# Weights that stream past the tokens: another matmul form for four products of a decoder layer

## The chip, the cores and the metric

The kernel runs on one core of a Trainium2 chip. The metric is the device time of one execution in microseconds (us), as the median of several runs. The core's engines work side by side, each through its own list of instructions in order: TensorE (PE) multiplies, VectorE (DVE) and ScalarE (ACT) do elementwise work, GpSimd (POOL) too, and SyncE (SP) issues most transfers from memory. Engines wait for each other by semaphores alone.

## The reference

One decoder layer for 256 tokens of 2048 features, in float32. A combined projection of the tokens gives the inputs of two branches and two merge gates; both branches are projected back, gated, added, projected once more and normalised:

```python
proj = x @ w_in        # columns: q_lat, c_kv, attn_gate, q_idx, k_idx, w_idx, x_rnn, rnn_gate, g_a, g_b
attn = sparse_attention(q_lat, rmsnorm(c_kv), q_idx, k_idx, w_idx, rel_bias, w_uv)   # 64 keys of each query
branch_a = (attn * silu(attn_gate)) @ w_branch_a
h = rglru(conv4(x_rnn), ...)                                                        # a scan over the tokens
branch_b = (h * silu(rnn_gate)) @ w_branch_b
merged = sigmoid(g_a) * branch_a + sigmoid(g_b) * branch_b
out = layernorm(2 ** 0.25 * x + merged @ w_out, ln_g, ln_b)
```

Here g_a and g_b are 2048 columns each, and w_branch_a, w_branch_b and w_out are 2048 x 2048.

## The kernel before, in words

Every large matrix product is made of float32 values split in two: a high part (`hi_of`, line 84, on ACT: a rounded copy) and the rest, the low part (`lo_of`, line 87, on DVE: value minus high part). A product is high x high + high x low + low x high. The tokens' two parts stand side by side in `xs`: for each of 16 blocks of 128 features, 256 columns of high parts and 256 of low ones.

The kernel has three phases. In the first, `load_a` and `split_a` (lines 223 and 234) bring the tokens and 848 columns of weights in 16 steps k, and PE multiplies as they come. In the second, `col_jobs` (line 51) lists 132 tiles of 128 weight columns: qi (indexer queries), ag (attention gate), q (latent queries), ga (gate A), ba (branch A's product), xr, gb, rg, bb (branch B's product). The weights of a tile come as two halves of 512 KB; `load_to` and `split_to` run some halves ahead, with 4 buffers for raw halves and 5 for split ones. In a tile the 128 weight columns are the stationary operand and the tokens move: a matmul with the weights' high part moves 512 columns (both halves of `xs`), one with the low part 256. `mm12` (line 192) issues a quarter of a tile, 4 of the 16 feature blocks: high first in the even quarters, low first in the odd ones. The result has features on the partitions and its two halves still have to be added, by `evac`: a copy on ACT, an addition on DVE.

After each quarter, a "tick", `tick` runs what is due of the work between the products: it is written as generators (`post_ga`, `post_bb`, `head`, `scores`, ...) which are called again some ticks later, so their instructions stand among the others of each engine at fixed places. `rel` copies a 4 MB table of position biases, dz, in the gate stage.

In the third phase the output projection has the other form: the tokens are stationary, 512 weight columns move, and `products` (line 781) issues three matmuls of 512 columns for one feature block and one half of the tokens. The result has tokens on the partitions. Its tiles are pso for the first three quarters of the columns, psz for the last one, which is done for one half of the tokens after the other, for the second half in two pieces of 256. `residual` adds the layer's input and `normalise` (line 800) finishes the norm of 128 tokens: the root of the variance by `rsqrt`, then `centre` (minus mean, times gain) and `finish` (times root, plus bias), with a quarter of the columns on ACT and POOL.

Of the kernel before, what the change touches and what calls it, by code (L numbers as in the profile page):

```python
# [49 lines left out]

def col_jobs():
# [12 lines left out]
def layer(ctx, tc, ar, out):  # L64
    nc = tc.nc
    jobs = col_jobs()
    NJ = len(jobs)
    at = {j: i for i, j in enumerate(jobs)}
# [34 lines left out]
    def gate_tile(name):  # L103
        return gt.tile([P, T], F32, name=name, tag="gate", bufs=32)
# [36 lines left out]

    halves = [("t", j, s) for j in range(NJ) for s in range(2)]
    halves += [("o", ec, pc) for ec in range(4) for pc in range(8)]
    NO = 2 * NJ
# [3 lines left out]
    def load_to(n):  # L148
        while st["load"] < min(n, len(halves)):
# [33 lines left out]
    def mm3(ps, hi, lo, rhs, first, last):  # L183

        if last:
            nc.tensor.matmul(ps[:, :T], lo, rhs[:, :T], start=first, stop=False)
            nc.tensor.matmul(ps, hi, rhs, start=False, stop=True)
        else:
            nc.tensor.matmul(ps, hi, rhs, start=first, stop=False)  # L189
            nc.tensor.matmul(ps[:, :T], lo, rhs[:, :T], start=False, stop=False)  # L190

    def mm12(ps, hi, lo, rhs, qt):


        def some(w, cols):
            for k in range(4 * qt, 4 * qt + 4):
                c = slice((k % 8) * P, (k % 8 + 1) * P)
                nc.tensor.matmul(ps[:, :cols], w[:, c], rhs[k][:, :cols], start=k == 0 and w is hi,  # L198
                                 stop=k == KT - 1 and w is hi)

        order = [(hi, 2 * T), (lo, T)]
        for w, cols in order if qt % 2 == 0 else order[::-1]:
            some(w, cols)
# [16 lines left out]
    with pool("pha", side="right") as pha:  # L220
# [13 lines left out]
        def split_a(k):  # L234
# [12 lines left out]
        nc.gpsimd.dma_start(params, ar["params"])  # L247
        nc.gpsimd.dma_start(causal, ar["causal"])
        nc.gpsimd.dma_start(kvg, ar["kvg"].to_broadcast([P, DL]))
        nc.gpsimd.dma_start(relb, ar["relb"])  # L250
        sp = {0: split_a(0)}
        for k in range(KT):
            if k + 1 < KT:
                sp[k + 1] = split_a(k + 1)
            if k + 4 < KT:
                load_a(k + 4)
            else:
                load_to(st["load"] + 1)
            hi, lo = sp.pop(k)
# [8 lines left out]
            for i in range(4):  # L268
                c = slice(A_Q + i * P, A_Q + (i + 1) * P)
                mm3(psq[i], hi[:, c], lo[:, c], xs[:, k, :], *fl)  # L270
# [214 lines left out]
    def head(h):  # L485
# [56 lines left out]
        nc.vector.tensor_mul(u, s, gates.pop(("ag", h)))  # L542
# [9 lines left out]
    def post_ag(i, ps):  # L552
        g = gate_tile(f"ag{i}")
        s = yield from evac(ps, f"ag{i}")
        yield
        nc.scalar.activation(g, s, AF.Sigmoid)
        yield
        nc.gpsimd.tensor_mul(g, g, s)
        gates["ag", i] = g

    def post_ga(i, ps):
        g = gate_tile(f"ga{i}")
        s = yield from evac(ps, f"ga{i}")
        yield
        nc.scalar.activation(g, s, AF.Sigmoid)
        gates["ga", i] = g

    def post_gb(i, ps):
        g = gate_tile(f"gb{i}")
        yield from evac(ps, f"gb{i}", dst=g)  # L570
        gates["gb", i] = g

    def post_ba(d, ps):
        s = yield from evac(ps, f"ba{d}")
        g = gates["ga", d]
        nc.vector.tensor_mul(g, g, s)

    def post_bb(d, ps):
        g = gates.pop(("gb", d))
        nc.scalar.activation(g, g, AF.Sigmoid)  # L580
        s = yield from evac(ps, f"bb{d}")
        yield
        nc.vector.tensor_mul(g, g, s)
        nc.vector.tensor_add(g, g, gates.pop(("ga", d)))
        yield
        hi_of(xs[:, d, :T], g)
        yield
        lo_of(xs[:, d, T:], g, xs[:, d, :T])
# [121 lines left out]
    E0, D0, A0, C0, G0 = (4 * at[k, 0] for k in ("ag", "q", "ga", "xr", "gb"))  # L710
# [19 lines left out]
    FIN = 4 * at["bb", 4]  # L730


    for j, (kind, i) in enumerate(jobs):
        rhs = us if kind in ("ba", "bb") else {k: xs[:, k, :] for k in range(KT)}
        ps = acc_tile(f"ps_{kind}{i}")
        for qt in range(4):
            t = 4 * j + qt
# [21 lines left out]
            hi, lo = parts[t // 2]  # L759
            mm12(ps, hi, lo, rhs, qt)  # L760
# [6 lines left out]
        spawn(4 * j + 4, posts[kind](i, ps))  # L767
# [31 lines left out]

    def normalise(t, ne):  # L800
# [31 lines left out]
        finish(cuts[0])  # L832
        centre(cuts[2])
        finish(cuts[1])
        centre(cuts[3])
        finish(cuts[2])
        finish(cuts[3])
# [82 lines left out]
```

## Time and profile before

| | |
|---|---|
| time, median of 3 runs | 1042.71 us (1040.66 to 1043.19) |
| the profiled execution | 1039.67 us, of which the span is 1037.8 us |
| PE busy | 1021.8 us, 98% of the span |
| DVE, ACT, POOL busy | 68%, 55%, 8% |
| mean granted clock of PE | 0.997 of full speed |
| transfers | 201 MB, mean 194 GB/s |

The span runs from the first instruction to the last. A matmul's length in the timeline is from its start to its result; since matmuls overlap, the pace is read from start to start. A row of the timeline can hold several equal instructions (x8). The bracket at a row's end is the idle time of the engine before it and what ended it.

### The profile page before, as it was taken

To read this page: it belongs to the slowest core of one execution; us is meant where nothing else is said; L and a number is where in the kernel's file an instruction comes from. 1 tells how busy PE (TensorE), PEld (TensorE's weight loads), DVE (VectorE), ACT (ScalarE), POOL (GpSimd) and SP (SyncE) were. 2 spreads that over 40 slices of the span, in tenths; PEclk is the share of its full clock that TensorE was granted. 3 is DMA by queue.
4 is the path that set the end of the run, shared out by engine and by line. 5 is a ranking of instruction groups with operands and counts; after the bars stand their busy time and mean duration, and the time that the engine had idled before them with its cause. 6 is when DMAs were issued, how large, how long until landed. Compare 5 with 4: busy or idle time off the path is not lost.

```text
span 1037.8 us, 16087 instructions
## 1 busy us (share of the span) xinstructions
PE 1021.8 (98%) x5944; PEld 901.4 (87%) x5944; DVE 709.8 (68%) x1246; ACT 571.1 (55%) x989; POOL 86.3 (8%) x121
## 2 busy tenths in 40 slices
PE   8999999999999999999999999999999999999995
PEld 8888888888898888888888888888888888888885
DVE  5668587777676766554555788856578877675666
ACT  5566355655656557544444555578755545554441
POOL 1003211211011100000000000000230020000002
PEclk9999999999999999999999999999999999999998
DMA  9745856755656654666665666556566577666642
GB/s 290 249 145 178 288 178 218 248 178 177 191 167 191 183 169 146 195 190 186 186 196 185 222 186 193 169 176 189 180 190 194 189 275 263 193 185 196 192 159 81
DMA packets 60574, 201.49 MB, mean 194 GB/s; under 512 B 6576, under 2 KB 13616, under 8 KB 59856
## 3 DMA queue, kind: packets, MB, share of 16 engines
q1 hardware_dynamic: 59120, 190.89, 59.1%
q0 software_dynamic: 944, 8.88, 2.3%
q8 instruction: 47, 0.77, 0.3%
q10 hardware_dynamic: 432, 0.70, 0.2%
q14 instruction: 31, 0.25, 0.1%
HBM read 198.31 MB, written 6.32 MB: 197 GB/s over the span
## 4 chain that ended last, share of the span: by engine, by line
PE 92%; DMA 3%; DVE 2%; ACT 1%; issue 1%; POOL 0%; SPq 0%; DVEq 0%; ACTq 0%; POOLq 0%
PE ps_q L198 17%; PE ps_ga L198 9%; PE ps_bb L198 9%; PE ps_rg L198 9%; PE ps_ba L198 9%; PE ps_gb L198 9%; PE ps_xr L198 9%; PE ps_ag L198 4%; DMA raw<-in_wt 3%; PE ps_qi L198 2%; PE pso L788 2%; PE pso L787 2%; PE pso L786 2%; ACT hi L85 1%; PE psq L189 1%
## 5 line engine op out<-in xcount | busy, mean ns | idle before, releaser
L89 DVE TENSOR_TENSOR lo<-raw,hi 128x1024 fp32r<-128x1024 f32 x324 | 401.3, 1239 | 290.7 <-ACT hi L85 289.4
L85 ACT ACTIVATE hi<-raw 128x1024 fp32r<-128x1024 f32 x324 | 340.7, 1052 | 104.0 <-PE pso L788 29.3
L198 PE MATMUL ps_q<-xs,hi 128*128 128x512 f32 x512 | 133.6, 394 | 0.0
L198 PEld LDWEIGHTS ps_q<-xs,hi 128*128 128x128 f32 x512 | 90.2, 189 | 14.2
L198 PEld LDWEIGHTS ps_q<-xs,lo 128*128 128x128 f32 x512 | 70.6, 190 | 5.1
L198 PE MATMUL ps_q<-xs,lo 128*128 128x256 f32 x512 | 73.5, 282 | 0.0
L198 PE MATMUL ps_ag<-xs,hi 128*128 128x512 f32 x256 | 66.1, 394 | 0.0
L198 PE MATMUL ps_ga<-xs,hi 128*128 128x512 f32 x256 | 65.5, 393 | 0.0
L198 PE MATMUL ps_gb<-xs,hi 128*128 128x512 f32 x256 | 64.4, 392 | 0.0
L198 PE MATMUL ps_rg<-xs,hi 128*128 128x512 f32 x256 | 64.3, 392 | 0.0
L198 PE MATMUL ps_ba<-ua,hi 128*128 128x512 f32 x256 | 64.3, 392 | 0.0
L198 PE MATMUL ps_bb<-ub,hi 128*128 128x512 f32 x256 | 64.3, 392 | 0.0
L198 PE MATMUL ps_xr<-xs,hi 128*128 128x512 f32 x256 | 64.0, 391 | 0.0
L198 PEld LDWEIGHTS ps_rg<-xs,hi 128*128 128x128 f32 x256 | 46.0, 189 | 8.2
L198 PEld LDWEIGHTS ps_bb<-ub,hi 128*128 128x128 f32 x256 | 46.0, 189 | 8.2
L198 PEld LDWEIGHTS ps_ba<-ua,hi 128*128 128x128 f32 x256 | 46.0, 189 | 8.2
L198 PEld LDWEIGHTS ps_gb<-xs,hi 128*128 128x128 f32 x256 | 46.0, 189 | 8.2
L198 PEld LDWEIGHTS ps_xr<-xs,hi 128*128 128x128 f32 x256 | 46.0, 188 | 8.0
L198 PEld LDWEIGHTS ps_ag<-xs,hi 128*128 128x128 f32 x256 | 45.3, 189 | 8.5 <-issue 0.9
L198 PEld LDWEIGHTS ps_ga<-xs,hi 128*128 128x128 f32 x256 | 45.6, 189 | 7.7
L442 POOL TENSOR_TENSOR bias<-bias,mask 128x256 f32<-128x256 f32 (+1 forms) x32 | 25.9, 830 | 174.8 <-DMA bias<-dz 136.2
L198 PEld LDWEIGHTS ps_xr<-xs,lo 128*128 128x128 f32 x256 | 35.8, 190 | 2.5
(270 smaller groups left out, 1810.2 us busy)
## 6 DMA issues: line engine op xcount, KB each, us to landing
raw<-in_wt SPq DMA_DIRECT2D x296, 512.0 KB, 4.3
raw<-in_wo SPq DMA_DIRECT2D x32, 512.0 KB, 3.6
wr<-in_wA SPq DMA_DIRECT2D x15, 424.0 KB, 4.8
dz<-dv POOLq DMA_DIRECT2D x1, 4096.0 KB, 18.3
bias<-dz SPq DMA_DIRECT2D x16, 256.0 KB, 4.5
xr<-in_xT SPq DMA_DIRECT2D x16, 128.0 KB, 4.3
uvr<-in_wuv SPq DMA_DIRECT2D x8, 256.0 KB, 4.2
wgr<-in_wg SPq DMA_DIRECT2D x4, 512.0 KB, 4.6
```

The source lines that it names most:

```text
L85: nc.scalar.activation(hi, src, AF.Copy)
L89: nc.vector.tensor_sub(lo, src, f(hi))
L189: nc.tensor.matmul(ps, hi, rhs, start=first, stop=False)
L198: nc.tensor.matmul(ps[:, :cols], w[:, c], rhs[k][:, :cols], start=k == 0 and w is hi, stop=k == KT - 1 and w is hi)
L442: nc.gpsimd.tensor_add(b[:, r, :W[r]], b[:, r, :W[r]], mask[:, r, :W[r]])
L786: nc.tensor.matmul(o, mh, hi, start=d == 0, stop=False)
L787: nc.tensor.matmul(o, mh, lo, start=False, stop=False)
L788: nc.tensor.matmul(o, ml, hi, start=False, stop=d == KT - 1)
```

## The change

The products ga, ba, gb and bb become 4 jobs of 512 columns each (`CHUNKS`), in the output projection's form: a job is 16 ticks, and a tick is one feature block with three matmuls for each half of the tokens. Their results have tokens on the partitions and need no halves added: `post_ga` takes the sigmoid straight from PSUM. What bb makes has to be turned for the output projection: `post_bb` has 8 transposes for each job on PE, and then the split into `xs`. The tiles that are left issue 8 high, 8 low, 8 low, 8 high matmuls (`mm`). Gate B stands ahead of rg as one block, and rg directly ahead of bb.

In the first phase four small loads (params 64 KB, causal 256 KB, kvg 128 KB, relb 2 KB) go from POOL's queue at the start to SP's at k = 8 to 11, the split of k = 1 and 2 is done in two pieces like that of k = 0, and the four 128-column products of a step take 4 high, then 4 low matmuls. In the third phase the residual of the second 128 tokens is written into PSUM in place and read there by the norm, which takes its columns in the pieces of the projection.

```diff
-    jobs += [("ga", i) for i in range(16)] + [("ba", i) for i in range(16)]
+    jobs += [("ga", i) for i in range(4)] + [("ba", i) for i in range(4)]
     jobs += [("xr", i) for i in range(16)]
-    jobs += [("gb", i) for i in range(14)] + [("rg", i) for i in range(16)] + [("gb", 14), ("gb", 15)]
-    jobs += [("bb", i) for i in range(16)]
+    jobs += [("gb", i) for i in range(4)] + [("rg", i) for i in range(16)]
+    jobs += [("bb", i) for i in range(4)]
...
-            for c in ([slice(0, A_Q), slice(A_Q, NA)] if k == 0 else [slice(0, NA)]):
+            for c in ([slice(0, A_Q), slice(A_Q, NA)] if k < 3 else [slice(0, NA)]):
...
-        nc.gpsimd.dma_start(params, ar["params"])
-        nc.gpsimd.dma_start(causal, ar["causal"])
-        nc.gpsimd.dma_start(kvg, ar["kvg"].to_broadcast([P, DL]))
-        nc.gpsimd.dma_start(relb, ar["relb"])
+        smalls = [(params, ar["params"]), (causal, ar["causal"]), (kvg, ar["kvg"].to_broadcast([P, DL])),
+                  (relb, ar["relb"])]
...
+            if 8 <= k < 12:
+                nc.sync.dma_start(*smalls[k - 8])
...
+    def post_ga(i, pss):
+        for t in range(2):
+            g = gates["ga", i, t] = gate_tile(f"ga{i}_{t}")
+            nc.scalar.activation(g, pss[t], AF.Sigmoid)
+            yield
...
+    def post_bb(i, pss):
+
+        gs = [gates.pop(("gb", i, t)) for t in range(2)]
+        for t in range(2):
+            nc.vector.tensor_mul(gs[t], gs[t], pss[t])
+            nc.vector.tensor_add(gs[t], gs[t], gates.pop(("ga", i, t)))
+            yield
+        yield
+        for e in range(2):
+            ps = aux_tile(f"psm{i}_{e}").rearrange("p (d s) -> p d s", d=2)
+            for d in range(2):
+                for t in range(2):
+                    c = slice((2 * e + d) * P, (2 * e + d + 1) * P)
+                    nc.tensor.transpose(ps[:, d, t * P:(t + 1) * P], gs[t][:, c], ident)
+            yield
+            d = slice(4 * i + 2 * e, 4 * i + 2 * e + 2)
+            hi_of(xs[:, d, :T], ps)
+            lo_of(xs[:, d, T:], ps, xs[:, d, :T])
...
+            if chunk:
+                for e in range(2):
+                    products(ps[e], parts[t // 2], qt % 2, qt, rhs[qt], e)
+            else:
+                high = qt in (0, 3)
+                w = parts[t // 2][0 if high else 1]
+                for kk in range(8):
+                    k = qt // 2 * 8 + kk
+                    mm(ps, w[:, kk * P:(kk + 1) * P], xs[:, k, :], high, k == 0 and high, k == KT - 1 and high)
...
     def residual(t, c, e, ps):
-        nc.vector.scalar_tensor_tensor(y[t][:, c], y[t][:, c], ALPHA, ps, op0=OP.mult, op1=OP.add)
-        nc.vector.bn_stats(st6[t][:, e, :], y[t][:, c])
+
+        to = ps if t else y[t][:, c]
+        nc.vector.scalar_tensor_tensor(to, y[t][:, c], ALPHA, ps, op0=OP.mult, op1=OP.add)
+        nc.vector.bn_stats(st6[t][:, e, :], to)
+        rows.append((t, c, to))
```

A tile on PE, in the xr stage (xr2 is its third tile, hi172 and lo172 the two parts of its first half of weights, x8 eight of a row). Before:

```order
L198 MATMUL ps_xr2_6327<-xs_93,hi172_6235 128x512 x4
L198 MATMUL ps_xr2_6327<-xs_93,lo172_6236 128x256 x8
L198 MATMUL ps_xr2_6327<-xs_93,hi172_6235 128x512 x4
L198 MATMUL ps_xr2_6327<-xs_93,hi173_6260 128x512 x4
L198 MATMUL ps_xr2_6327<-xs_93,lo173_6261 128x256 x8
L198 MATMUL ps_xr2_6327<-xs_93,hi173_6260 128x512 x4
```

and now:

```order
L203 MATMUL ps_xr2_5899<-xs_93,hi172_5809 128x512 x8
L203 MATMUL ps_xr2_5899<-xs_93,lo172_5810 128x256 x8
L203 MATMUL ps_xr2_5899<-xs_93,lo173_5833 128x256 x8
L203 MATMUL ps_xr2_5899<-xs_93,hi173_5832 128x512 x8
L203 MATMUL ps_xr3_5963<-xs_93,hi174_5859 128x512 x8
```

The two runs of low matmuls now stand together, and with the next tile so do two runs of high ones.

The bb stage on PE. Before, at its first tile (ub0 to ub7 are the scan's gated results of feature blocks 0 to 7, the moving operand; hi264 and lo264 the weights, stationary):

```order
L198 MATMUL ps_bb0_9172<-ub0_8275,hi264_9073 128x512
L198 MATMUL ps_bb0_9172<-ub1_8333,hi264_9073 128x512
L198 MATMUL ps_bb0_9172<-ub2_8391,hi264_9073 128x512
L198 MATMUL ps_bb0_9172<-ub3_8449,hi264_9073 128x512
L198 MATMUL ps_bb0_9172<-ub0_8275,lo264_9074 128x256
L198 MATMUL ps_bb0_9172<-ub1_8333,lo264_9074 128x256
L198 MATMUL ps_bb0_9172<-ub2_8391,lo264_9074 128x256
L198 MATMUL ps_bb0_9172<-ub3_8449,lo264_9074 128x256
L198 MATMUL ps_bb0_9172<-ub4_8507,lo264_9074 128x256
L198 MATMUL ps_bb0_9172<-ub5_8565,lo264_9074 128x256
L198 MATMUL ps_bb0_9172<-ub6_8623,lo264_9074 128x256
L198 MATMUL ps_bb0_9172<-ub7_8681,lo264_9074 128x256
```

Now, in the second job, where the first job's transposes stand (psm0_0; gb0_0 and gb0_1 are the gated sums of the first job for the two halves of the tokens):

```order
L756 MATMUL ps_bb1_1_8713<-hi273_8664,ub3_7935 128x512
L757 MATMUL ps_bb1_1_8713<-lo273_8665,ub3_7935 128x512
L758 MATMUL ps_bb1_1_8713<-hi273_8664,ub3_7935 128x512
L601 MATMUL psm0_0_8766<-ident_81,gb0_0_7093 128x128
L601 MATMUL psm0_0_8766<-ident_81,gb0_1_7109 128x128
L601 MATMUL psm0_0_8766<-ident_81,gb0_0_7093 128x128
L601 MATMUL psm0_0_8766<-ident_81,gb0_1_7109 128x128
L756 MATMUL ps_bb1_0_8712<-hi274_8682,ub4_7993 128x512
L757 MATMUL ps_bb1_0_8712<-lo274_8683,ub4_7993 128x512
L758 MATMUL ps_bb1_0_8712<-hi274_8682,ub4_7993 128x512
L756 MATMUL ps_bb1_1_8713<-hi274_8682,ub4_7993 128x512
L757 MATMUL ps_bb1_1_8713<-lo274_8683,ub4_7993 128x512
```

The weights are the moving operand now, the low matmuls have 512 columns too, and four transposes stand between two steps.

The last norm on DVE, second half of the tokens (mv1 holds mean and variance, lt1 the root, gb0 and gb1 gain and bias, y1 the rows in SBUF). Before, from the first centre on:

```order
L810 SCALAR_TENSOR_TENSOR y1_9388<-y1_9388,mv1_10045,gb0_9389 128x384
L290 RECIPROCAL lt1_10047<-lt1_10047 128x1
L810 SCALAR_TENSOR_TENSOR y1_9388<-y1_9388,mv1_10045,gb0_9389 128x512
L292 TENSOR_TENSOR lt1_10047<-lt1_10047 128x1
L293 TENSOR_TENSOR lt1_10047<-lt1_10047 128x1
L294 SCALAR_TENSOR_TENSOR lt1_10047<-lt1_10047 128x1
L814 SCALAR_TENSOR_TENSOR y1_9388<-y1_9388,lt1_10047,gb1_9390 128x384
L810 SCALAR_TENSOR_TENSOR y1_9388<-y1_9388,mv1_10045,gb0_9389 128x384
L814 SCALAR_TENSOR_TENSOR y1_9388<-y1_9388,lt1_10047,gb1_9390 128x512
L810 SCALAR_TENSOR_TENSOR y1_9388<-y1_9388,mv1_10045,gb0_9389 128x256
L814 SCALAR_TENSOR_TENSOR y1_9388<-y1_9388,lt1_10047,gb1_9390 128x384
L814 SCALAR_TENSOR_TENSOR y1_9388<-y1_9388,lt1_10047,gb1_9390 128x256
```

and now:

```order
L836 SCALAR_TENSOR_TENSOR pso0_1_9229<-pso0_1_9229,mv1_9225,gb0_8720 128x512
L292 RECIPROCAL lt1_9227<-lt1_9227 128x1
L294 TENSOR_TENSOR lt1_9227<-lt1_9227 128x1
L295 TENSOR_TENSOR lt1_9227<-lt1_9227 128x1
L296 SCALAR_TENSOR_TENSOR lt1_9227<-lt1_9227 128x1
L839 SCALAR_TENSOR_TENSOR y1_8719<-pso0_1_9229,lt1_9227,gb1_8721 128x512
L836 SCALAR_TENSOR_TENSOR pso1_1_9394<-pso1_1_9394,mv1_9225,gb0_8720 128x512
L839 SCALAR_TENSOR_TENSOR y1_8719<-pso1_1_9394,lt1_9227,gb1_8721 128x512
L836 SCALAR_TENSOR_TENSOR psz1_0_9802<-psz1_0_9802,mv1_9225,gb0_8720 128x256
L839 SCALAR_TENSOR_TENSOR y1_8719<-psz1_0_9802,lt1_9227,gb1_8721 128x256
L836 SCALAR_TENSOR_TENSOR psz1_1_9853<-psz1_1_9853,mv1_9225,gb0_8720 128x256
L839 SCALAR_TENSOR_TENSOR y1_8719<-psz1_1_9853,lt1_9227,gb1_8721 128x256
```

The rows are read from the projection's own PSUM tiles (pso0_1, pso1_1, psz1_0, psz1_1), and after the first piece each finish stands right behind its centre.

## Rows read from the trace of the kernel before

**Rows 1.** The page: busy time of each engine, and the chain by engine.

```profile
PE 1021.8 (98%) x5944; PEld 901.4 (87%) x5944; DVE 709.8 (68%) x1246; ACT 571.1 (55%) x989; POOL 86.3 (8%) x121
...
PE 92%; DMA 3%; DVE 2%; ACT 1%; issue 1%; POOL 0%; SPq 0%; DVEq 0%; ACTq 0%; POOLq 0%
```

**Rows 2.** Timeline of PE in the bb stage: start us, length us, operation, count.

```profile
881.78 2.00 PE L198 MATMUL ps_bb<-ub,hi 128*128 128x512 f32 x8
...
883.62 1.12 PE L198 MATMUL ps_bb<-ub,lo 128*128 128x256 f32 x8
...
926.47 2.00 PE L198 MATMUL ps_bb<-ub,hi 128*128 128x512 f32 x8
```

**Rows 3.** Tile pso on PE: duration min/median/max ns, first and last start.

```profile
L786 PE MATMUL pso<-hi,xs x96: 389/389/393, 938.6 to 1003.2; 128*128 128x512 f32 x96
...
L788 PE MATMUL pso<-hi,xs x96: 389/389/389, 939.0 to 1003.6; 128*128 128x512 f32 x96
```

**Rows 4.** Timeline of PE in the ga stage, around three transposes.

```profile
403.39 0.27 PE L517 MATMUL pspT<-ident,lg 128*128 128x128 f32 x1
403.50 0.38 PE L519 MATMUL pspT<-ident,lg 128*128 128x128 f32 x2
403.64 1.17 PE L198 MATMUL ps_ga<-xs,hi 128*128 128x512 f32 x4
404.65 1.10 PE L198 MATMUL ps_ga<-xs,lo 128*128 128x256 f32 x8
```

**Rows 5.** Timeline of DVE in the gate stage, behind the copy dz.

```profile
126.34 1.23 DVE L89 TENSOR_TENSOR lo<-raw,hi 128x1024 fp32r<-128x1024 f32 x1 [7.54 <-ACT hi L85]
```

**Rows 6.** Waits of PE's weight loads: us in total, times, longest.

```profile
PEld ps_ag L198 <- DVE lo L89: 1.0, 2, 0.5
```

**Rows 7.** Timeline of the first 16 us, ACT, DVE and PE; idle time in brackets.

```profile
3.60 0.48 ACT L85 ACTIVATE ahi<-wr 128x336 fp32r<-128x336 f32 x1 [0.37 <-DMA wr<-in_wA]
...
4.11 0.51 DVE L89 TENSOR_TENSOR alo<-wr,ahi 128x336 fp32r<-128x336 f32 x1 [0.43 <-ACT ahi L85]
...
8.07 0.91 ACT L85 ACTIVATE ahi<-wr 128x848 fp32r<-128x848 f32 x1 [2.06 <-DMA wr<-in_wA]
...
9.03 0.42 PE L265 MATMUL psc<-ahi,xs 128*128 128x336 f32 x1 [1.07 <-ACT ahi L85]
...
10.11 0.42 PE L266 MATMUL psc<-alo,xs 128*128 128x336 f32 x1 [0.66 <-DVE alo L89]
...
14.94 0.32 PE L265 MATMUL psc<-ahi,xs 128*128 128x336 f32 x1
```

**Rows 8.** Window of the first 13 us: busy us by engine, clock, DMA share, GB/s.

```profile
0.00:13.00 13.00, 10.29 (x63) 9.13 (x64) 4.93 (x11) 6.81 (x12) 3.07 (x10) 1.00 0.86 281
```

**Rows 9.** Timeline around step k = 14 of the first phase.

```profile
38.24 1.06 ACT L85 ACTIVATE hi<-raw 128x1024 fp32r<-128x1024 f32 x1 [3.72 <-DMA raw<-in_wt]
...
41.90 0.42 PE L266 MATMUL psc<-alo,xs 128*128 128x336 f32 x1 [1.02 <-DVE alo L89]
```

**Rows 10.** Timeline of DVE and POOL from PE's last matmul on.

```profile
1026.45 0.42 DVE L791 SCALAR_TENSOR_TENSOR y<-y,psz 128x256 f32<-128x256 f32 x1 [0.85 <-PE psz L788]
...
1028.42 0.73 DVE L810 SCALAR_TENSOR_TENSOR y<-y,mv,gb 128x512 f32<-128x512 f32 x1
1028.74 1.56 POOL L821 TENSOR_TENSOR y<-y,gb 128x512 f32<-128x512 f32 x1 [5.80 <-ACT y L820]
1029.07 1.24 DVE L292 TENSOR_TENSOR lt<-lt 128x1 f32<-128x1 f32 x1
...
1031.80 1.75 DVE L814 SCALAR_TENSOR_TENSOR y<-y,lt,gb 128x512 f32<-128x512 f32 x1
...
1033.87 1.00 DVE L814 SCALAR_TENSOR_TENSOR y<-y,lt,gb 128x384 f32<-128x384 f32 x2
```

**Rows 11.** Line 281 on DVE, gate tiles: count, duration min/median/max ns.

```profile
L281 DVE TENSOR_TENSOR s_ag<-ps_ag,r_ag x16: 401/412/417, 85.5 to 175.8; 128x256 f32<-128x256 f32 x16
```

**Rows 12.** The page: the split on DVE, count, busy us, mean ns.

```profile
L89 DVE TENSOR_TENSOR lo<-raw,hi 128x1024 fp32r<-128x1024 f32 x324 | 401.3, 1239 | 290.7 <-ACT hi L85 289.4
```

More of the change, by code (lines that the diff above doesn't have):

```diff
@@ L66, in layer @@
     jobs = col_jobs()
-    NJ = len(jobs)
-    at = {j: i for i, j in enumerate(jobs)}
+    at, end = {}, 0
+    for job in jobs:
+        at[job] = end
+        end += ticks(job)
     def pool(name, side=None, **kw):
@@ L139, in layer @@
     dz = dram.tile([P, NH, VL], F32, name="dz")
-    halves = [("t", j, s) for j in range(NJ) for s in range(2)]
-    halves += [("o", ec, pc) for ec in range(4) for pc in range(8)]
-    NO = 2 * NJ
+    tiles = [job for job in jobs if job[0] not in CHUNKS]
+    halves = []
+    for job in jobs:
+        if job[0] in CHUNKS:
+            halves += [("w" + job[0], job[1], pc) for pc in range(8)]
+        else:
+            halves += [("wt", tiles.index(job), s) for s in range(2)]
+    NO = len(halves)
+    halves += [("wo", ec, pc) for ec in range(4) for pc in range(8)]
     raws, parts = {}, {}
@@ L181, in split_to, with mm @@
             st["split"] += 1
[L183 to L203, printed above, removed]
+    def mm(ps, w, rhs, high, start, stop):
+        n = 2 * T if high else T
+        nc.tensor.matmul(ps[:, :n], w, rhs[:, :n], start=start, stop=stop)
     def mm6(o, pairs):
@@ L267, in layer @@
                 nc.tensor.matmul(o, x_lo, hi[:, :A_Q], start=False, stop=fl[1])
-            for i in range(4):
-                c = slice(A_Q + i * P, A_Q + (i + 1) * P)
-                mm3(psq[i], hi[:, c], lo[:, c], xs[:, k, :], *fl)
+            last = k == KT - 1
+            for high in (False, True) if last else (True, False):
+                for i in range(4):
+                    w = (hi if high else lo)[:, A_Q + i * P:A_Q + (i + 1) * P]
+                    mm(psq[i], w, xs[:, k, :], high, fl[0] and high, last and high)
             if k >= 12:
@@ L729, in layer, with products @@
         spawn(G0 + 50 + q, roots(q))
-    FIN = 4 * at["bb", 4]
-    for j, (kind, i) in enumerate(jobs):
+    for i in range(4):
+        spawn(at["bb", i] + 4, gate_bb(i))
+    FIN = at["bb", 1]
+    def products(o, w, i, d, xd, t, c=slice(0, 512)):
+        hi, lo = (p[:, c] for p in (w[i] if isinstance(w, list) else [p[:, i * 512:(i + 1) * 512] for p in w]))
+        mh = xd[:, t * P:(t + 1) * P]
+        ml = xd[:, T + t * P:T + (t + 1) * P]
+        nc.tensor.matmul(o, mh, hi, start=d == 0, stop=False)
+        nc.tensor.matmul(o, mh, lo, start=False, stop=False)
+        nc.tensor.matmul(o, ml, hi, start=False, stop=d == KT - 1)
+    for kind, i in jobs:
         rhs = us if kind in ("ba", "bb") else {k: xs[:, k, :] for k in range(KT)}
-        ps = acc_tile(f"ps_{kind}{i}")
-        for qt in range(4):
-            t = 4 * j + qt
+        chunk = kind in CHUNKS
+        ps = [acc_tile(f"ps_{kind}{i}_{t}") for t in range(2)] if chunk else acc_tile(f"ps_{kind}{i}")
+        for qt in range(ticks((kind, i))):
+            t = at[kind, i] + qt
             if t == D0:
@@ L831, in normalise @@
         nc.scalar.dma_start(out[t * P:(t + 1) * P, rest], yr)
[L832 to L837, printed above, removed]
+        finish(*mine[0])
+        for m in mine[1:]:
+            centre(*m)
+            finish(*m)
     t0 = 2 * NO
     for ec in range(3):
-        pss = [acc_tile(f"pso{ec}_{t}") for t in range(2)]
+        pss = [acc_tile(f"pso{ec}_0"), aux_tile(f"pso{ec}_1")]
         for pc in range(8):
```

119 lines of the change are left out of this document (51 added, 68 removed).

## The prediction

> **What bounds the kernel now.** I read the page first: TensorE (PE) is busy for 98% of the span and is 92% of the chain that ended last [rows 1]. So only four things can move the end: the pace of PE's stream, PE work added or taken out, the places where PE waits, and the tail after its last matmul. The timeline of PE in a steady stretch gives the pace. There, 8 matmuls of 512 columns ("high": both halves of the tokens) take 1.84 us and the 8 of 256 ("low") behind them 0.95 us; 16 such periods last 926.47 - 881.78 = 44.69 us, 2.793 each [rows 2]. The same stream of 512 columns alone is in the output projection: 288 matmuls, first start 938.6, last 1003.6, so 65.0 / 287 = 226.5 ns each [rows 3]. I then looked for PE's own waits (start, one pair of stalls in the gate stage) and for the tail.
>
> **Gates and branch products (ga, ba, gb, bb): 64 tiles become 16 chunks.** Before, a tile is 16 high and 16 low matmuls, two periods: 64 x 2 x 2.793 = 357.5 us. After, a chunk is 16 steps of 6 matmuls of 512 columns in the form of the output projection: 16 x 16 x 6 = 1536 x 0.2265 = 347.9 us. The columns streamed are the same; 256-column matmuls at 0.119 (0.95 / 8) cost more than half of 0.2265, and a high matmul behind low ones costs 1.84 / 8 = 230. Gain 9.6 us. I take the output projection's pace because operation, shapes and split are the same there, and its weights are split beside it just as here. Bounds: 223 ns, as little below the row's as 230 lies above it, to 230 ns, the pace of mixed runs: gain 15 to 4.
>
> A rule of the Trainium skill speaks against this gain. The row: 119 ns for 256 columns, 226.5 for 512. "TensorE: Matmul & The Clock Gate", section "Back-to-back issue gap", gives columns / 2.4 + 2.5 ns on a warm engine, an estimate of 109 and 216; by it the four stages would save only 2.5 ns for each of the 512 matmuls fewer (2048 before, 1536 now), an estimate of 1.3 us. The trace has 10 ns more than either figure, and 10 ns on 256 columns weigh twice as much as on 512; I go by the rows.
>
> **Transposes added.** The new bb result has tokens on the partitions and the output projection needs features there, so each of 4 bb jobs adds 8 transposes of 128x128, 32 in all, on PE. The nearest rows: three such transposes and the 4 high matmuls behind them take 404.65 - 403.39 = 1.26 us, 4 high alone 0.92, so 0.34 / 3 = 0.11 each with the restart [rows 4]. Loss 32 x 0.115 = 3.7 us; bounds 3 (no restart) to 9 (each one's whole 0.27).
>
> The Trainium skill says on the same page, "TensorE: Matmul & The Clock Gate", in "Part 4: PE-mode transpose", that one costs about 275 ns in a kernel. By that the loss would be an estimate of 8.8 us; in this trace 0.27 is a transposition's own duration and they start 0.11 apart.
>
> **Tiles (qi, ag, q, xr, rg: 84 jobs).** 8 high, 8 low, 8 low, 8 high makes runs of 16 where there were runs of 8, so the second 8 high go at 226.5 instead of 230: 8 x 230 - 8 x 226.5 = 0.028 us per tile, less some for the products inserted between them. Gain 84 x 0.021 = 1.8 us; bounds 0 and 3.
>
> That order has a price. The second half of a tile now begins with its low part, 4 x 0.23 = 0.92 us sooner than before; the first half uses it later. It matters only where the low part arrives just in time: the 4 MB copy dz holds the weights back until DVE idles 7.54 us at 126.34, and PE's weight loads wait twice for "lo" in that stage, 1.0 us in all [rows 5, 6]. One shift by 0.92 ends the shortage, since DVE makes up no time and loses none. Loss 0.6 us, bounds 0 and 2.
>
> **First loads.** Four small transfers (450 KB) leave the POOL queue at the start and go on SP's at k = 8 to 11; for k = 1, 2 the split is made in two pieces. Now PE, free at 7.96, waits 1.07 and 0.66 us at k = 1: the weights are there at 8.07, where ACT had idled 2.06, then ACT needs 0.91 and DVE a little more; the first 336 columns of k = 0 took 0.48 and 0.51 [rows 7]. Without the 450 KB (1.6 us at the 281 GB/s of this stretch [rows 8]; I count 1.0 of it, since they end behind k = 1) and with the pieces, the two parts are there at 7.6 and 8.1, so the second matmul of k = 1 starts at 8.1 instead of 10.11. From it to k = 3 now take 14.94 - 10.11 = 4.83 us, so k = 3 starts near 12.9. Against this: at k = 14 PE waits 1.02 us because ACT sat 3.72 us behind the first raw tile [rows 9]; SP now issues the small ones ahead of it, and a PE that is 2 us early reaches this wait earlier. Up to 1.2 us of the gain may go there; I keep 1.9. Bounds 0.3 and 2.4. SP has the small ones behind its waits for wr buffers; nothing needs them before the scores, far later.
>
> **The last norm.** For the second half of the tokens the residual stays in PSUM and is read there. DVE idles 0.85 us until PE's last product, then 8.4 us of DVE work run to 1034.87, with the store behind. Two DVE operations are held by a POOL one on the same SBUF data: 1.24 us for a 128x1 and 1.75 for a 512 [rows 10]. Unheld, a 512 takes 0.73. The 16 DVE additions that read the gate tiles from PSUM all lie within 401 to 417 ns, though POOL multiplied in that stage too [rows 11]. So the second hold (1.0 us) goes; the first stays, since the small products of the root are still in SBUF. Each finish now stands directly behind its centre, which costs some 0.1 for each of 3, and a fourth piece costs no more columns but an extra start, 0.15. Gain 0.5; bounds +0.5 (nothing gained, a dependent wait) and -1.9 (both holds gone).
>
> **What comes free beside PE.** Chunks need no high and low halves added, so 64 copies on ACT and as many additions on DVE go. PE did not wait for them: worth nothing. If ACT or DVE fell behind, that would be PE's loss.
>
> **Sum.** -9.6 + 3.7 - 1.8 + 0.6 - 1.9 - 0.5 = -9.5 us. The profiled execution took 1039.67 (span 1037.8 and 1.9 around it), so 1030.2; the median of the runs is 1042.71, 3.0 more, and the same difference gives 1033.2.
>
> **Rivals.**
> 1. Waits take part of it: PE waits for the transposes' data. In bb PE has 4 steps of 1.36 us between a job's end and the first transpose, 5.4 us; DVE does in that time 4 operations of 512 at up to 0.73 and a split, some 4.2. Behind one more split (1.24 [rows 12]) it is equal. Were DVE 1.2 us late in all 4 jobs, 4.8 us are lost: 1038.0. For it: DVE is in order. Against: DVE loses 64 additions, and the chain shows it at 2%.
> 2. The stream gains nothing: what makes 256-column matmuls and mixed runs dear is not their form but the splits and loads beside them, so that the chunks cost the 357.5 of before. Sum +0.1, 1042.8: no change. For it: by columns the work is equal. Against: the output projection's 226.5, with the same splits beside [rows 3].
> 3. Slower: PE restarts at every new piece of weights in the chunks. A chunk streams what ACT and DVE wrote, and the first two matmuls of each half wait for them, one for the high part and one for the low. A restart shows behind the transposes: 4 high matmuls take 404.65 - 403.64 = 1.01 us there, 0.09 over 4 x 0.23 [rows 4]. In 16 chunks of 8 halves with 2 waits that is 256 x 0.09 = 23.0 us, the sum becomes +13.5, the time 1056.2. It decides from 9.5 / 256 = 0.037 us a wait on. For it: two waits within 0.23 us. Against: the output projection has the same waits, and its 226.5 holds them.
> 4. The change does not do what it says at the start: the start's gain is given back whole at k = 14. Then 1035.1; it is inside the forecast's range.
>
> **Chances.** Forecast with rival 4 inside it 0.76, rival 1 0.12, rival 2 0.07, rival 3 0.05. All small terms at their good ends make it 3.2 us less, 1030.0; all at their bad ends, the transposes aside, 5.8 more, 1039.0; the runs before spread over 2.5 us. To hold 8 in 10 I take 1028.5 to 1039.5, which takes in rival 1. A measurement of this kernel tells from no change what is over 0.3%, 3.1 us. Faster 0.86 (the forecast, most of rival 1), same 0.09 (rival 2 and part of rival 1), slower 0.05 (rival 3).
>
> **What would show it.** In the profile after: 6 matmuls of a chunk step at 1.36 us, each of ga, ba, gb and bb near 87 us; bb with groups of 4 transposes of some 0.45 us and no idle PE before them; k = 3 of the first phase starting near 12.9; PE's wait for "lo" in the gate stage up to 1 us longer in sum; from the last matmul to the last DVE operation 0.5 us less. Wrong would be: a chunk's matmuls over 230 ns apart, PE idle before transposes, or a wait at k = 14 that grew by 2 us.

## The result, and the profile after

The changed kernel takes 1032.2 us (4 runs, 1030.91 to 1033.08) against 1042.74 (4 runs, 1040.66 to 1043.19): ratio 0.9902, interval 0.9885 to 0.9919. In a later set of runs (e9) it took 1032.62 us against 1039.89, ratio 0.9929 (0.9914 to 0.9944). The forecast was 1033.2, with a range of 1028.5 to 1039.5. The two profiled executions lie only 7.1 us apart (1039.67 and 1032.58): that of before was faster than each of its four runs above, that of after lies near its median. So the traces account for 7.1 us, stage by stage from the first matmul of each to the next stage's first:

| stage, us | before | after | difference | after with paced last loads (e12) |
|---|---|---|---|---|
| start to qi | 46.59 | 42.75 | -3.84 | 43.51 |
| ag | 97.76 | 98.44 | +0.68 | 98.53 |
| q | 217.10 | 216.62 | -0.48 | 216.61 |
| ga | 95.91 | 93.80 | -2.11 | 93.81 |
| ba | 89.39 | 87.04 | -2.35 | 87.04 |
| gb and rg | 180.83 | 178.37 | -2.46 | 178.37 |
| bb | 89.38 | 92.24 | +2.86 | 89.88 |
| pso | 65.29 | 66.21 | +0.92 | 66.22 |
| last matmul to the end | 11.67 | 11.36 | -0.31 | 11.06 |

qi, xr and psz are within 0.05 of before. The page of the changed kernel, busy time and chain, answers to [rows 1]: PE is still 98% busy, with 480 matmuls fewer.

```profile
PE 1014.5 (98%) x5464; PEld 880.0 (85%) x5464; DVE 683.2 (66%) x1150; ACT 550.8 (53%) x909; POOL 83.9 (8%) x117
...
PE 93%; DVE 2%; ACT 1%; DMA 1%; issue 1%; POOL 0%; ACTq 0%; DVEq 0%; POOLq 0%
```

The tile of the ba chunks on PE (count, duration min/median/max ns, first and last start) answers to [rows 2, 3]: 384 matmuls, first start 474.9, last 561.7, so 86.8 / 383 = 226.6 ns each, the output projection's pace.

```profile
L756 PE MATMUL ps_ba<-hi,ua x128: 389/389/389, 474.9 to 561.2; 128*128 128x512 f32 x128
...
L758 PE MATMUL ps_ba<-hi,ua x128: 389/389/389, 475.3 to 561.7; 128*128 128x512 f32 x128
```

The timeline of PE at the transposes of bb's job 0 (start us, length us; idle time and its releaser in brackets):

```profile
865.81 0.33 PE L601 MATMUL psm<-ident,gb 128*128 128x128 f32 x1
868.26 0.55 PE L601 MATMUL psm<-ident,gb 128*128 128x128 f32 x3 [2.13 <-DVE gb L593]
...
870.03 0.60 PE L601 MATMUL psm<-ident,gb 128*128 128x128 f32 x4
870.38 0.48 PE L756 MATMUL ps_bb<-hi,ub 128*128 128x512 f32 x1
870.70 0.39 PE L757 MATMUL ps_bb<-lo,ub 128*128 128x512 f32 x1
```

The second transpose starts 2.45 us behind the first: PE waits for DVE's addition. An undisturbed group of four takes 870.38 - 870.03 = 0.35 us, and the matmul behind it 0.32 instead of 0.227: 0.44 a group, 3.5 us for all eight (the forecast, from [rows 4], was 3.7). The other three jobs have no such wait. DVE in that stretch, and the four loads of 1 MB that POOL issued 22 us earlier:

```profile
859.45 1.23 DVE L100 TENSOR_TENSOR lo<-raw,hi 128x1024 fp32r<-128x1024 f32 x1 [2.54 <-ACT hi L96]
863.21 1.22 DVE L100 TENSOR_TENSOR lo<-raw,hi 128x1024 fp32r<-128x1024 f32 x1 [2.53 <-ACT hi L96]
...
865.67 1.22 DVE L100 TENSOR_TENSOR lo<-raw,hi 128x1024 fp32r<-128x1024 f32 x1
866.81 0.68 DVE L592 TENSOR_TENSOR gb<-gb,ps_bb 128x512 f32<-128x512 f32 x1
867.52 0.69 DVE L593 TENSOR_TENSOR gb<-gb,ga 128x512 f32<-128x512 f32 x1
```
```profile
842.97 0.61 POOL L784 DMA_DIRECT2D gb<-in_lng  x1 [91.42 <-DVE ri L711]
843.57 0.53 POOL L785 DMA_DIRECT2D gb<-in_lnb  x1
844.10 1.04 POOL L787 DMA_DIRECT2D y<-in_xres  x2
```

and the weights' loads by SP from 843 to 850 in this kernel:

```profile
L174 SPq DMA_DIRECT2D raw<-in_wbb x3: 327/328/328, 844.4 to 849.4; - x3
...
DMA to landing us min/median/max: 10.1/11.6/12.6
```

DVE idles 2.5 us twice for a split whose weights took 10.1 to 12.6 us to land; the multiply and add that the transposes need stand behind these splits in DVE's order.

Waits of PE's weight loads (total, times, longest), answering to [rows 6]: the gate stage's wait grew from 1.0 to 2.0 us.

```profile
PEld psm L601 <- DVE gb L593: 2.6, 2, 2.3
PEld ps_ag L203 <- DVE lo L100: 2.0, 2, 1.6
```

The first phase, ACT and PE, answering to [rows 7]: ACT has k = 1's weights at 6.76 (8.07 before), PE does not wait there; k = 3 starts at 12.46 (14.94). This execution was a lucky one: its qi starts earliest of the ten traces with the new loads (after, e2, e4, e5 and e7 to e12), and PE still waits 0.4 to 1.2 us at k = 1 in six of them, e9's of this same kernel among these. The window of the first 13 us (PE busy 10.29 before, [rows 8]):

```profile
6.76 1.01 ACT L96 ACTIVATE ahi<-wr 128x336 fp32r<-128x336 f32 x2 [1.61 <-DMA wr<-in_wA]
```
```profile
7.97 0.32 PE L266 MATMUL psc<-alo,xs 128*128 128x336 f32 x1
...
12.46 0.32 PE L265 MATMUL psc<-ahi,xs 128*128 128x336 f32 x1
```
```profile
0.00:13.00 13.00, 12.03 (x78) 11.45 (x79) 7.22 (x16) 8.62 (x17) 0.68 (x6) 1.00 0.87 291
```

The tail on DVE and POOL, answering to [rows 10]: the 128x1 operation is still held (1.12 us), the 512 beside the second POOL operation is not (0.75; 1.75 before).

```profile
1019.65 0.43 DVE L813 SCALAR_TENSOR_TENSOR psz<-y,psz 128x256 f32<-128x256 f32 x1 [0.92 <-PE psz L758]
...
1022.08 1.12 DVE L295 TENSOR_TENSOR lt<-lt 128x1 f32<-128x1 f32 x1
...
1024.88 0.75 DVE L839 SCALAR_TENSOR_TENSOR y<-pso,lt,gb 128x512 f32<-128x512 f32 x1
...
1026.98 0.48 DVE L839 SCALAR_TENSOR_TENSOR y<-psz,lt,gb 128x256 f32<-128x256 f32 x1
```
```profile
1024.28 1.26 POOL L854 TENSOR_TENSOR y<-y,gb 128x512 f32<-128x512 f32 x1 [1.10 <-ACT y L853]
```

### The profile page after: what moved, and what is told of

Read it like the earlier page. It is cut to its first block, busy times and chain, and to the rows that moved or that the text cites. A ratio compares the mean times of both kernels' runs of the same rounds, so it can differ in the third digit from the quotient of the medians.

```text
span 1030.7 us, 14867 instructions
## 1 busy us (share of the span) xinstructions
PE 1014.5 (98%) x5464; PEld 880.0 (85%) x5464; DVE 683.2 (66%) x1150; ACT 550.8 (53%) x909; POOL 83.9 (8%) x117
## 4 chain that ended last, share of the span: by engine, by line
PE 93%; DVE 2%; ACT 1%; DMA 1%; issue 1%; POOL 0%; ACTq 0%; DVEq 0%; POOLq 0%
PE ps_q L203 17%; PE ps_rg L203 9%; PE ps_xr L203 9%; PE ps_ag L203 6%; PE ps_ga L756 3%; PE ps_gb L758 3%; PE ps_ga L757 3%; PE ps_ga L758 3%; PE ps_ba L757 3%; PE ps_ba L756 3%; PE ps_gb L756 3%; PE ps_gb L757 3%; PE ps_ba L758 3%; PE psq L203 2%; PE ps_bb L756 2%; PE ps_qi L203 2%
## 5 line engine op out<-in xcount | busy, mean ns | idle before, releaser
L203 PE MATMUL ps_q<-xs,hi 128*128 128x512 f32 x512 | 122.4, 391 | 0.0
L203 PE MATMUL ps_ag<-xs,hi 128*128 128x512 f32 x256 | 61.5, 391 | 0.0
L756 PE MATMUL ps_bb<-hi,ub 128*128 128x512 f32 x128 | 50.4, 394 | 0.0
L756 PE MATMUL ps_ga<-hi,xs 128*128 128x512 f32 x128 | 50.0, 391 | 0.0
L758 PE MATMUL ps_ga<-hi,xs 128*128 128x512 f32 x128 | 49.9, 390 | 0.0
L758 PE MATMUL ps_gb<-hi,xs 128*128 128x512 f32 x128 | 49.9, 390 | 0.0
L758 PE MATMUL ps_bb<-hi,ub 128*128 128x512 f32 x128 | 49.9, 389 | 0.0
L757 PE MATMUL ps_gb<-lo,xs 128*128 128x512 f32 x128 | 49.8, 389 | 0.0
L757 PE MATMUL ps_ga<-lo,xs 128*128 128x512 f32 x128 | 49.8, 389 | 0.0
L757 PE MATMUL ps_bb<-lo,ub 128*128 128x512 f32 x128 | 49.8, 389 | 0.0
L756 PE MATMUL ps_ba<-hi,ua 128*128 128x512 f32 x128 | 49.8, 389 | 0.0
L757 PE MATMUL ps_ba<-lo,ua 128*128 128x512 f32 x128 | 49.8, 389 | 0.0
```

Source lines behind the costliest of these rows:

```text
L203: nc.tensor.matmul(ps[:, :n], w, rhs[:, :n], start=start, stop=stop)
```

## Experiments

Theory: the time is PE's stream, with a better pace of the chunks, plus the waits that the change adds or removes at the start, in the gate stage and before bb's transposes. Rival: the chunks' gain is smaller, and the edits at the start and end carry the rest. Each ratio is to the kernel before on the same chip.

**e1: the chunks and transposes alone.** The tile order, the first loads and the last norm as before (the three edits of e2 to e4 together, and the old order of the four 128-column products in the first phase, which no run takes back alone: a step there takes 2.34 us in either order, 38.16 to 40.50 before and 38.04 to 40.38 after).

> Only the chunks of ga, ba, gb and bb with their transposes; tile order, first loads, psq order and last norm as in the kernel before. My theory (the parts add up, and the chunks carry most): ga and ba stages at about 93.8 and 87.0 us as in the changed kernel (95.9 and 89.4 before), bb about 92 with its transposes; the start of the qi stage back near 46.6; the whole 1036.5, that is 6 below the kernel before and some 4.5 above the changed one. Rival (the start carries the gain, the chunks give little once transposes and their wait are paid): 1039 or more.

Measured 1036.86 us, 0.9956 (0.9941 to 0.9971), beside 1040.93 for before. By the median the chunks with their transposes bring -4.1 us, near what I expected (1036.5) and clear of the rival's 1039. The trace has ga -2.1, ba -2.4 and gb -2.1 us as in the changed kernel, and the wait before bb's transposes here too (2.2 us).

**e2: the old order inside a tile.**

```diff
-                high = qt in (0, 3)
-                w = parts[t // 2][0 if high else 1]
-                for kk in range(8):
...
+                for high in (True, False) if qt % 2 == 0 else (False, True):
+                    w = parts[t // 2][0 if high else 1]
+                    for k in range(4 * qt, 4 * qt + 4):
```

> The changed kernel with the tiles' old order: 4 high, 4 low, 4 low, 4 high of a quarter each. My theory: the runs of 8 cost the tile stages some 1.5 us again (q 217.1 instead of 216.6, ag's own stream 0.4), but PE's wait for the low part in the gate stage falls from 1.6 + 0.3 us to below 0.5, because the second half of a tile begins with its high part again; net +0.5, 1032.7, not to be told from the changed kernel. Rival (the order is worth the 1.8 us of the forecast, the wait has another cause and stays at 1.6): 1034.

Measured 1033.09 us, 0.9922 (0.9905 to 0.9939). q takes 217.10 and rg 89.39 again, against 216.62 and 89.07 with the new order, which so gains 0.5 and 0.3 there and nothing in qi and xr. The time lies between my theory's and the rival's and tells them not apart. The gate stage's waits fell less than I expected: PE waits there 1.5 us for low parts and 0.7 for high ones; ag is no shorter (98.59).

**e3: the old first loads**, small ones on POOL's queue and only k = 0 in two pieces.

```diff
-            for c in ([slice(0, A_Q), slice(A_Q, NA)] if k < 3 else [slice(0, NA)]):
+            for c in ([slice(0, A_Q), slice(A_Q, NA)] if k == 0 else [slice(0, NA)]):
...
+        for small in smalls:
+            nc.gpsimd.dma_start(*small)
...
-            if 8 <= k < 12:
-                nc.sync.dma_start(*smalls[k - 8])
```

> The changed kernel with the four small loads on POOL's queue at the start again, and the split in two pieces for k = 0 alone. My theory: PE waits at k = 1 and k = 2 again (2.3 us with its restarts) and at k = 14 (1.2 us), the qi stage starts near 46.6 instead of 42.75; 1036.0. Rival (the k = 14 wait went by chance, from run to run): qi near 45.2, 1034.5.

Measured 1036.22 us, 0.9945 (0.9928 to 0.9962): some 3 us of the gain are the first loads'. The trace is of its fastest run (1032.96; the others 1034.70 to 1036.71), so it does not show all of them. The qi stage starts at 46.05; PE waits for k = 1 and then runs slowly:

```profile
8.58 0.42 PE L265 MATMUL psc<-ahi,xs 128*128 128x336 f32 x1 [1.69 <-ACT ahi L96]
9.65 0.42 PE L266 MATMUL psc<-alo,xs 128*128 128x336 f32 x1 [0.65 <-DVE alo L100]
...
10.55 1.91 PE L203 MATMUL psq<-xs,ahi 128*128 128x512 f32 x4
```
```profile
10.55:13.70 3.15, 3.15 (x12) 2.77 (x12) 1.97 (x3) 2.57 (x5) 0.00 (x0) 0.50 1.02 378
```

The last three columns are the granted clock, the DMA share and GB/s. The clock is 0.50, that is 1.2 instead of 2.4 GHz, for 3.1 us, half of which are lost (an estimate). k = 14 has no wait this time, which fits the rival's view that it comes by chance.

**e4: the old last norm**, the residual in SBUF, pieces of 384, 512, 384 and 256, and each centre ahead of the finish before it.

```diff
-        to = ps if t else y[t][:, c]
-        nc.vector.scalar_tensor_tensor(to, y[t][:, c], ALPHA, ps, op0=OP.mult, op1=OP.add)
+        nc.vector.scalar_tensor_tensor(y[t][:, c], y[t][:, c], ALPHA, ps, op0=OP.mult, op1=OP.add)
```

> The changed kernel with the norm of before (second half's rows in SBUF, its four cuts). My theory: from PE's last matmul to the last DVE operation 8.7 us again instead of 8.1, one 512-wide operation held to 1.75 us by POOL; 0.3 to 0.6 us, 1032.7. Rival (the store behind it sets the end whatever DVE does): 1032.2, no change of the span from the last matmul on.

Measured 1033.14 us, 0.9925 (0.991 to 0.9941); from the last matmul to the end 11.99 us. Tails with the old norm are 11.67, 11.69 and 11.99, with the new one 11.05 to 11.41: about 0.5 us. The second hold is back:

```profile
1024.87 1.75 DVE L834 SCALAR_TENSOR_TENSOR y<-y,lt,gb 128x512 f32<-128x512 f32 x1
```

If the parts add, the changed kernel on this chip would take (1033.09 + 1036.22 + 1033.14 - 1036.86) / 2 = 1032.8 us, and its parts are chunks with transposes -4.1, first loads -3.4, last norm -0.3, tile order -0.3, each with an uncertainty of over 1 us. So whether the chunks or the first loads brought more, these runs do not tell.

**e5: the transposes four steps later.**

```diff
-        yield
+        yield 4
         for e in range(2):
             ps = aux_tile(f"psm{i}_{e}").rearrange("p (d s) -> p d s", d=2)
```

> The 8 transposes of a branch or gate job are queued four steps later, behind more products of the next tile. Mine: the wait of 2.45 us before job 0's transposes in bb (waits of 0.8 to 2.5 us in the runs so far) goes, because the low part of y then stands complete when TensorE reaches them; bb takes about 89.8 us instead of 92.2, and the kernel about 1030.5 us. Rival: the weights of that job themselves come late, so the wait only moves to the next low part; bb stays at 92 us and the kernel at 1032 to 1033 us.

Measured 1031.38 us, 0.9901 (0.9888 to 0.9913). The wait is gone and went nowhere else: bb takes 89.88 us. (The transposes read the gated sums of L593, not a low part, as my expectation has it.) The time is not measurably below the changed kernel's; its start was among the late ones (qi at 44.76).

**e6: the small loads back on POOL's queue**, the two pieces kept for k = 1 and 2 (of e3's edit the last two parts).

> The small constant loads go back to the start of GpSimd's queue; the split of the first pieces stays. Mine: the small loads' removal carries about half of the start's gain: PE waits about 1 us again at k=1 or 2, the qi stage starts near 44.5 us instead of 42.75, the kernel takes about 1034 us. Rival: the split pieces carry all of it: qi starts at 42.8 us, about 1032.5 us.

Measured 1034.71 us, 0.9943 (0.9926 to 0.9961), runs from 1032.94 to 1037.89. The time speaks for my theory, the trace not clearly: qi starts at 44.45, but in ten traces with the new loads it starts anywhere from 42.75 to 44.76 (mean 43.6; with the old loads 44.62, 46.05 and 46.59). How the gain divides between the two edits stays open.

**e7: chunk products of 256 columns.**

```diff
+                    for x, w in ((mh, hi), (mh, lo), (ml, hi)):
+                        for c in (slice(0, 256), slice(256, 512)):
+                            nc.tensor.matmul(ps[e][:, c], x, w[:, c], ...
```

> Each chunk product streams its 512 weight columns as two matmuls of 256 columns with the same tokens as weights of the array: 3072 matmuls instead of 1536. Mine: a 256-column matmul costs 119.5 ns as in the kernel before's tiles, so the chunks take 3072 x 0.1195 = 367 us instead of 348, and the kernel about 1051 us. Rival: what a matmul costs beyond its columns is 2.5 ns, and the rest of the 226.5 ns is the columns' own: 1536 more matmuls cost 3.8 us, about 1036 us.

Measured 1050.34 us, 1.0084 (1.0071 to 1.0097): mine. The ba tile's matmuls on PE:

```profile
L794 PE MATMUL ps_ba<-hi,ua x512: 283/283/283, 477.7 to 569.8; 128*128 128x256 f32 x171
```

768 matmuls from 477.7 to 569.8, 120.1 ns each; two make 240 where one of 512 columns takes 226.6. Operands and neighbouring work are the same, so the cost goes with the split into smaller matmuls. Each matmul has a weight load of its own, so there are twice as many of these too; which of the two costs the time is not separated. The Trainium skill's "TensorE: Matmul & The Clock Gate", section "Back-to-back issue gap", gives 2.5 ns beyond the columns for an isolated matmul at the full clock; the measured split costs some 13.5 ns each time, and the measurement decides.

**e8: later transposes, and ag tiles whose second half is 4 high, 4 low, 4 low, 4 high.**

```diff
+                if kind == "ag" and qt > 1:
+                    runs = [(high, range(4 * qt, 4 * qt + 4)) for high in ((True, False) if qt == 2 else (False, True))]
```

> The later transposes, and in the gate stage's ag tiles the second half of the products taken as 4 high, 4 low, 4 low, 4 high instead of 8 low, 8 high, so that a late low part is needed later. Mine: the waits for DVE's low parts in the gate stage (1.9 us above the pace in the changed kernel) fall by about 0.9 us, the additional turns from high to low cost 0.3 us: about 0.5 us below the kernel with late transposes alone, near 1030 us. Rival: the gate stage is held by its DMAs, and the wait moves to the next product: the same time as with late transposes alone.

Measured 1030.87 us, 0.9899 (0.9885 to 0.9912): the same as e5 by the intervals. The waits of PE in ag:

```profile
PEld ps_ag L203 <- DVE lo L100: 1.0, 2, 0.5
PEld ps_ag L203 <- ACT hi L96: 0.6, 1, 0.6
```

Low parts are waited for 1.0 us, as in the kernel before, but 0.6 for a high part comes instead. ag takes 97.85 us; e5, without the edit, had 97.60. The wait moved, as the rival says; that the stage is held by its DMAs is not shown.

**e9: the changed kernel again**, beside the next two.

> The changed kernel as it is, beside the next two on one chip. 1032 us, with the wait of about 2.4 us before job 0's transposes in bb, and the qi stage starting between 42.7 and 44.8 us, as the chance of the start has it.

Measured 1032.62 us (1031.70 to 1033.99), 0.9929; the wait before the transposes is 1.4 us here instead of 2.4, qi starts at 44.43.

**e10: the last loads spread over bb on POOL's queue.**

```diff
+            if t - FIN in (0, 8, 16, 24):
+                nc.gpsimd.dma_start(*last_loads[(t - FIN) // 8])
```

> The changed kernel with its four 1 MB loads for the last norm (lng, lnb and two halves of xres) issued 8 pairs of products rows apart through bb's jobs 1 to 3 (some 11 us each), not all at job 1's start. Mine: these loads delay the weights of job 1, which stand ahead of job 0's multiply and add in DVE's order; spread, the weights land within 6 us of their issue, the wait before job 0's transposes goes below 0.5 us, and the kernel takes about 2 us less than the changed kernel, near 1030.3 us. Rival: DVE is late through its own work (multiply, add and low parts of one job in a row), and the loads have no part in it: wait and time stay at 2.4 and 1032 us.

Measured 1032.61 us, 0.993 (0.9915 to 0.9945); the wait is 1.1 us. This settles nothing between the theory and the rival, since the loads were not spread. POOL in this kernel:

```profile
843.42 0.61 POOL L787 DMA_DIRECT2D gb<-in_lng  x1 [91.42 <-DVE ri L711]
844.03 0.54 POOL L787 DMA_DIRECT2D gb<-in_lnb  x1
844.55 1.04 POOL L787 DMA_DIRECT2D y<-in_xres  x2
```

POOL had nothing else to do in bb, so it ran through its list at once, whatever stood between in the program.

**e11: later transposes, e8's ag tiles and e10's edit together.**

> Later transposes, ag tiles with 4 high, 4 low, 4 low, 4 high in their second half, and the spread loads together. Mine: the wait that later transposes cover is the one that the spread loads remove, so the two don't add: about 2 us below the changed kernel, 1030 us, as each alone. Rival: the loads' spreading frees something more in bb (hidden waits for weights): 1 us further down, 1029 us.

Measured 1030.71 us (1030.59 to 1031.12), 0.9912 (0.9898 to 0.9926): every run below every run of e9 on the same chip, by 1.9 us in the median. With the loads not spread, that is what later transposes and ag's tiles bring together; the rival's 1029 did not come.

**e12: the last loads on SP's queue**, between the weights' loads; the transposes and tiles of the changed kernel.

```diff
-                nc.gpsimd.dma_start(gb[0], ar["lng"].to_broadcast([P, DM]))
...
+            if t - FIN in (0, 8, 16, 24):
+                nc.sync.dma_start(*last_loads[(t - FIN) // 8])
```

> The changed kernel with its four 1 MB loads for the last norm put into SyncE's queue, after every fourth load of weights in bb's jobs 1 to 3, where the wait of the weights' loads for a free buffer holds them apart (on GpSimd's own queue nothing held them: spread over the program they were still issued within 1.65 us). Mine: weights delayed by only 1 MB at a time land within 7 us of their issue, the wait before job 0's transposes (1.0 to 2.5 us in the runs so far with the changed kernel's transposes) goes below 0.3 us and bb's start-to-start is about 89.9 us, as with later transposes (89.65 to 89.88); the time about 1031 us. Rival: DVE is late through its own work, the wait stays above 0.8 us.

Measured 1030.33 us, 0.9894 (0.9878 to 0.991). The weights' loads from 843 to 856, the first two of the 1 MB loads on SP's queue, DVE's last addition for the transposes, and PE at the transposes:

```profile
L174 SPq DMA_DIRECT2D raw<-in_wbb x5: 327/328/328, 845.3 to 855.7; - x5
...
DMA to landing us min/median/max: 3.4/3.5/3.6
```
```profile
861.47 0.38 SPq L787 DMA_DIRECT2D gb<-in_lng  x1
...
874.62 0.42 SPq L787 DMA_DIRECT2D gb<-in_lnb  x1
```
```profile
864.38 0.69 DVE L593 TENSOR_TENSOR gb<-gb,ga 128x512 f32<-128x512 f32 x1
```
```profile
866.44 0.39 PE L758 MATMUL ps_bb<-hi,ub 128*128 128x512 f32 x1
866.67 0.60 PE L601 MATMUL psm<-ident,gb 128*128 128x128 f32 x4
867.02 0.48 PE L756 MATMUL ps_bb<-hi,ub 128*128 128x512 f32 x1
```

The 1 MB loads now stand 13 us apart, and the first is issued after these weights. Weights land in 3.5 us instead of 11.6, DVE's addition ends at 865.07, 1.6 us ahead of the transposes, these follow without a wait, and bb takes 89.88 us. So the loads were the cause; DVE's own work alone leaves no wait. This is the lowest median of all kernels here, but its interval overlaps those of e5, e8 and e11.

## Why the prediction came out

- **Chunks, -9.6.** Mechanism and pace as forecast (226.6 for 226.5 ns). In size: ga -2.11, ba -2.35, gb -2.14 (-2.46 with rg, less rg's 0.32), and bb, in e12, 89.88 less six groups of transposes (2.7) against 89.38, -2.2: together -8.8. Rival 2 (nothing gained) and rival 3 (a restart at each piece) are out: ga, ba and gb would have had no gain, or become 23.0 / 4 - 2.4 = 3.4 us longer each. My "each near 87 us" held for ba alone: ga (93.80) and gb (89.30) hold other products too, bb the transposes.
- **Transposes, +3.7.** 3.5 by their own rows, 3.8 by the stages: bb in e12 is 2.84 longer than ba, with six groups, and the other two stand in pso's stage (+0.92).
- **Rival 1** was real in one job of four, 0.8 to 2.5 us instead of 4.8, but for another reason than I gave. I had counted DVE's own work, 4.2 us in 5.4; e12 shows that this fits. What I left out is that POOL's four loads are issued at the start of job 1 and delay the weights whose splits stand ahead in DVE's order. They were in the trace of before as well, where nothing at that place waited for DVE. I gave the rival 0.12 and no part in the forecast; and PE idle before transposes is one of the signs that I had named for being wrong.
- **Tile order, -1.8.** 0.5 in q, 0.3 in rg, none in qi and xr. Probably the products inserted there break the runs, which I had allowed for only in part; no run tests it. In ag the stage's scatter is larger than the gain. By times 0.3.
- **Low part sooner, +0.6.** The wait for low parts in ag grew from 1.0 to 2.0 us; ag became 0.68 longer. Without the new order it was no shorter (98.59 in e2, 98.43 in e1), so the order hardly sets that stage's length, which scatters from 96.4 (e7) to 98.6 us.
- **First loads, -1.9.** The second matmul of k = 1 starts at 7.97 (forecast 8.1), k = 3 at 12.46 (12.9). The gain is larger, 2.2 us from the mean starts of qi and 3.4 by times. Rival 4 (given back at k = 14) came true in some executions only: that wait is 1.24 before, 0.56 in e4, 1.1 in e5, none in after and e3. What I lacked: a wait at k = 1 can also cost the clock (e3). The new loads remove that wait in four of ten traces and leave 0.4 to 1.2 us of it in six; and fewer of their runs have a lowered clock (last section).
- **Last norm, -0.5.** The hold that was to go went, the other stayed; from the last matmul's start to DVE's end 8.12 us instead of 8.74.

The sum of -9.5 stands between what the two sets of runs measured, -10.5 and -7.3 (1039.89 to 1032.62). That it came so near is in part luck, because errors offset each other: by the parts of e1 to e4 (-8.1 in all), chunks with transposes and their wait brought 1.8 less than the -5.9 forecast, the tile order 0.9 less than -1.2, the start 1.5 more. The base is less sure than I took it to be: the medians of the kernel before went from 1039.89 to 1042.74 over five sets of runs, from 1039.89 to 1041.77 on one and the same chip. In which stage its other runs lose up to 3 us over the profiled one stays open, since only that one has a trace; the granted clock has a part in it (last section). In the prediction's range the good ends of the small terms add up to 3.7 us (1.2, 0.6, 0.5, 1.4), not 3.2, which the range holds as well.

## What to carry to other kernels

A moving operand of 512 columns beats two of 256 when PE is the bound, by some 13.5 ns a pair here; read the pace from a stage that already has the form. Before a wait is added to PE, list what stands ahead of the awaited instruction in its engine's order, and ask of each whether its data can be late: here bulk loads on another queue delayed splits that stood ahead. A bulk load is paced by a queue that has to wait for something, not by its place in the program.

## What was not expected of the hardware

After e3's waits at k = 1 the granted clock was 0.50 for 3.1 us. In e1 it was 0.56 behind the 2.2 us wait at bb's transposes, in the changed kernel 1.00 behind 2.45 us of the same wait. Windows (us, busy by engine PE, PEld, DVE, ACT, POOL, clock, DMA share, GB/s), first of e1, then of the changed kernel:

```profile
868.60:870.80 2.20, 0.26 (x2) 0.00 (x0) 2.17 (x4) 0.00 (x0) 0.00 (x0) 1.00 0.79 236
870.80:874.40 3.60, 3.59 (x13) 2.91 (x14) 3.01 (x3) 1.55 (x2) 0.00 (x0) 0.56 0.75 226
```
```profile
865.80:868.20 2.40, 0.34 (x2) 0.14 (x1) 2.37 (x4) 0.21 (x1) 0.00 (x0) 1.00 0.85 232
868.30:872.00 3.70, 3.70 (x20) 3.14 (x21) 3.31 (x4) 2.66 (x4) 0.00 (x0) 1.00 0.76 231
```

The same wait can thus cost its own length or some 1.6 us more (bb without its wait takes 91.4 us in e1 and 89.8 in the changed kernel). What decides between the two was not tried.

Such stretches are a part of the spread between executions too. From e1 on each run has its mean granted clock on record, and so have the runs of the changed kernel. It is 0.995 in the two traced executions with a stretch at the lower level (e1, e3) and 0.996 or 0.997 in the twelve without one. With the first loads of before (before, e1, e3, e6) 40 of 60 runs lie at 0.995 or below, with the new ones 4 of 52. The kernel before takes 1042.2 us in the mean of its 11 runs at 0.993 or 0.994, and 1039.9 in that of its 13 at 0.996 or 0.997. So part of the first loads' gain is probably the clock, in runs that no trace shows; where in them it fell stays open.
